# A hybrid DiT block on one core: the scan's quad loop written as four overlapping steps, one stage put between merge and transpose, splits and modulation of the FFN norm issued earlier, and the last output rows regrouped

## The chip, the cores and the metric

The kernel runs on one core of a Trainium2 chip. The metric is the device time of one execution in microseconds; the time before is 1929.78 us, the median of three runs (1927.39 to 1932.99). The core has five engines with queues of their own: TensorE (PE in the profile, PEld for its weight loads), VectorE (DVE), ScalarE (ACT), GpSimd (POOL, not used here) and SyncE (SP, which issues nearly all DMAs). Each engine runs its instructions in the order in which the program lists them.

## The reference

One layer of a diffusion block on 256 latent tokens and 256 context tokens of width 2048, all float32:

```
hl = rmsnorm(x) * (1 + sc_m) + sh_m
p  = hl @ w_in                      # SSD columns | z | pool | Fourier | three gates
y_ssd  = rmsnorm_per_group(ssd(p) * silu(z)) @ w_ssd_out
y_pool = pool(p), y_four = fourier(p) @ w_fourier
x = x + g_m * ((s0 * y_pool + s1 * y_four + s2 * y_ssd) @ w_out)      # s = sigmoid(gates)
x = x + g_f * swiglu(rmsnorm(x) * (1 + sc_f) + sh_f)                  # 2048 -> 5632 -> 2048
out = rmsnorm(x)
```

`ssd` is a bidirectional Mamba-2 scan over 32 heads in 4 groups, in chunks of 128 tokens; its initial states come from the context tokens. The six modulation vectors (sc, sh, g, each for mixer and FFN) are `silu(c) @ w_ada + b_ada`. Of the context only the scan states are needed, so its projection stops at the SSD columns.

## The kernel before

**Stages.** The product of tokens and weights is cut into *stages*. A stage is one weight tile of 2 x 128 rows by 512 columns (512 KB) and, as a rule, 12 matmuls of 128x128x512. The precision of float32 is kept by splitting both operands in a high and a low part: `split` (L123) makes `hi` with an ACT cast (L124) and `lo = raw - hi` with a DVE subtraction (L125), and `mm3` (L130) issues three matmuls (L131 hi x hi, L132 lo x hi, L133 hi x lo). So each stage asks one DMA of SP, one cast of ACT, one subtraction of DVE and 12 matmuls of PE.

**The order.** Nothing reorders the program; its order is made at build time by `stream` (L198). For stage i it issues loads up to stage i + LEAD + 3 and splits up to stage i + LEAD (LEAD is 2), then the stage's matmuls, then a helping of side work. Loaded tiles go through five buffers (`raw`), shared by the weight tiles and by the tiles of `w_ada`; split parts go through three (`whi`, `wlo`), or, for a stage that is *held*, through the large pool H (`hhi`, `hlo`). A buffer is loaded anew when ACT and DVE have read it; a split begins when PE has finished the stage that used the same part buffer.

**Side work** consists of generators in a list (`beside`). `side(room)` (L187) adds `room` to a credit (at most 3), and lets each generator take one step while the credit is above 0.2; a step gives back its own estimate of DVE time (`yield 1.2`). `need(key)` (L179) runs a generator to its end at once. The modulation vectors past the first are side work as well: `plan_ada` (L514) attaches *units* (a 512 KB tile of `w_ada`, one DVE multiply-add of 128x1024, L461) to stages.

**The places of the change, in the order of time.**
- *Scan* (`ssd`, L648): for each group of 8 heads a quad loop (L750 to L788) runs over two blocks b of 4 heads and two chunks t. Each quad makes 16 small ACT multiplications (L745, tiles `rh`) and 4 more (L757, tile `W`), four matmuls that sum the decays (L761), an ACT exponential (L767), a DVE product `W*E` (L768), and four matmuls with the values (L772); each block then adds the skip term (L778), is transposed (L784) and added into `y` (L787). The steps of one quad follow each other, one per helping of side work.
- *norm_y* (L1050): the group norm of the scan's output, started by `start_norm` 14 stages before the stages with `w_ssd_out` (called phase q here, L1079).
- *Phase q*: for each of four column blocks n, eight stages of gate, eight of `w_ssd_out`, then `merge(2, n)` (L953; DVE, L963 and L967, tile `mg`) and `to_feature(n)` (L1088), which transposes the merged block on PE (L1095) and splits it (L1098 ACT, L1099 DVE). `turn_m` asks for the merge with `need` and goes straight on.
- *Phase o* (`w_out`) and the *FFN norm*: the last block of `w_out` is arranged so that rows t = 0 end first (`mm_first`), while rows t = 1 (`mm_second`) and the first gate stages (`mm_gate0`, `mm_gate1`) follow in halves. `norm_ffn` (L1126) gives a diagonal matrix with 1/rms; `turn(n)` (L1137) transposes and scales a block by it on PE (L1141), modulates it with four DVE multiply-adds (L1144, 128x128 each), and splits it into `h2h` and `h2l`.
- *Last rows* (`last_rows`, L1314): the final 512 rows of `w_ffn_down`, in 8 pieces (column block n, half p). Pieces of n < 3 multiply the rows t = 0 only; after the last piece, `mm_piece` does n = 3 of t = 0 (in two spans of 256 columns), `finish(0)` (final norm and store of t = 0), all four blocks of t = 1, and `finish(1)`.

Of the kernel before, what the change touches and what calls it, by code (L numbers as in the profile page):

```python
# [72 lines left out]
class Stage:  # L73


    def __init__(self, src, n, mm, first=None, room=1.45, held=False):
        self.src, self.n, self.mm, self.first, self.room, self.held = src, n, mm, first, room, held
        self.after, self.extra = [], []
        self.raw = self.parts = None
# [3 lines left out]
def hybrid_block(ctx: ExitStack, tc, io):  # L83
# [114 lines left out]
    def stream():  # L198
        while at["run"] < len(stages):
            i = at["run"]  # L200
            st = stages[i]
            load_upto(i + LEAD + 4)
# [445 lines left out]
    def ssd(g):  # L648
# [87 lines left out]
        def operands(b, t):  # L736

            h0 = 8 * g + 4 * b
            rhs = []
            for d, r in enumerate((LE, GE)):  # L740
                for a in (dah, dal):
                    rh = Q([P, 4, P], F32R, nme="rh")
                    av = a[:, t, 32 * d + h0 : 32 * d + h0 + 4].bitcast(F32)
                    for i in range(4):
                        S.activation(rh[:, i, :], r, AF.Copy, scale=av[:, i : i + 1])  # L745
                    rhs.append((gt_r if d == 0 else lt_r, rh))
            return rhs

        yps = [None, None]
        for b in range(2):  # L750
            h0 = 8 * g + 4 * b
            yps[b] = aux([P, 2, 256])
            for t in range(2):
                rhs = operands(b, t)
                W = Q([P, 4, P], nme="W")
                for i in range(4):
                    S.activation(W[:, i, :], cbf[:, t, :], AF.Copy, scale=ddt[:, t, h0 + i : h0 + i + 1])  # L757
                yield 0.0
                seg = aux([P, 4, P])
                for n, (m, rh) in enumerate(rhs):  # L760
                    T.matmul(seg, m, rh, start=n == 0, stop=n == 3)  # L761
                for i in range(4):
                    V.scalar_tensor_tensor(W[:, i, :], cbb[:, t, :], ddt[:, t, 32 + h0 + i : 33 + h0 + i], W[:, i, :],
                                           ALU.mult, ALU.add)
                yield 1.1
                E = Q([P, 4, P], nme="E")
                S.activation(E, seg, AF.Exp)  # L767
                V.tensor_tensor(W, W, E, ALU.mult)  # L768
                yield 0.6
                for i in range(4):  # L770
                    h = 4 * b + i
                    T.matmul(yps[b][(h % 2) * 64 : (h % 2) * 64 + 64, i // 2, t * P : (t + 1) * P],  # L772
                             xl[:, t, h * HD : (h + 1) * HD], W[:, i, :], start=True, stop=True)
            yield 0.0
# [5 lines left out]
            yield 0.8  # L780
# [4 lines left out]
            yield 0.0  # L785
            yv = y[g][:, :, 256 * b : 256 * b + 256]
            V.tensor_tensor(yv, yv, ps, ALU.add)  # L787
            yield 0.6  # L788
# [261 lines left out]
    def norm_y():  # L1050
        S.activation(zss, zss, AF.Sqrt, bias=eps4, scale=1.0 / CH)
# [36 lines left out]
    def to_feature(n):  # L1088
        mh[n], ml[n] = H([P, 4, 256], F32R, nme="fth"), H([P, 4, 256], F32R, nme="ftl")
        for i in range(2):  # L1090
# [5 lines left out]
            yield 0.0  # L1096
            s2 = slice(2 * i, 2 * i + 2)
            S.activation(mh[n][:, s2, :], ps, AF.Copy, scale=0.5)  # L1098
            V.scalar_tensor_tensor(ml[n][:, s2, :], ps, 0.5, mh[n][:, s2, :].bitcast(F32), ALU.mult, ALU.subtract)  # L1099
        yield 1.2  # L1100
# [25 lines left out]
    def norm_ffn(t):  # L1126
# [10 lines left out]
        def turn(n):  # L1137
# [4 lines left out]
            for c in range(4):  # L1142
                kt = 4 * n + c
                V.tensor_scalar(hf[:, c, :], ps[:, c, :], Af[:, kt : kt + 1], Sf[:, kt : kt + 1], ALU.mult, ALU.add)  # L1144
# [13 lines left out]
    def phase_o(n):  # L1158
# [127 lines left out]
    oss = C([P, 2, 5], nme="oss")  # L1286

# [26 lines left out]
    def last_rows():  # L1314
# [9 lines left out]
        def block(t, n, i, cs, p):  # L1324
            if p == 0:
                ps[0] = acc((P, cs.stop - cs.start))
            hi, lo = pieces[2 * n + p]
            op = pair_op(ah[10:11], al[10:11])
            for k in range(2):
                kt = 2 * p + k  # L1330
                mm3(ps[0], *op(kt, t), hi[:, k, cs], lo[:, k, cs], kt == 0, kt == 3)
# [4 lines left out]
            V.tensor_tensor(tmp[:, cs], ps[0], gf[n][:, n % 2, cs], ALU.mult)  # L1336
# [24 lines left out]
        def mm_piece(n, p):  # L1361
            def mm(parts):
                pieces.append(parts)
                if n < 3:
                    block(0, n, 0, slice(0, CH), p)
                    return
                if p == 0:
                    return
                for t in range(2):
                    for m in range(4) if t else (3,):  # L1370
                        for i, cs in spans(m):
                            for q in range(2):
                                block(t, m, i, cs, q)
                    finish(t)
            return mm

        for n in range(4):
            for p in range(2):
                add(rows(io["w_ffn_down"], 40 + 2 * p, 2, n * CH, CH), CH, mm_piece(n, p),
                    first=first if n + p == 0 else None, room=0.3, held=True)  # L1380
# [36 lines left out]
    def start_norm():  # L1417
        need("ssd", "z0", "z1", "z2", "z3")
        spawn("Y", norm_y(), True)
    s_q = len(stages)  # L1420
    stages[s_q - 14].after.append(start_norm)
# [22 lines left out]
    plan_ada(u_all[:40], s_u, s_q)  # L1444
    plan_ada(u_all[40:], s_q, s_o + 10)
# [85 lines left out]
```

## Time and profile before

| | |
|---|---|
| median of three runs | 1929.78 us |
| the profiled execution | 1927.37 us, of which the span of its instructions is 1925.6 us |
| mean granted TensorE clock | 0.989 |
| busy: PE / DVE / ACT | 96% / 64% / 46% of the span |
| read from HBM | 405.56 MB, 212 GB/s over the span |

The profile's rows give, for each engine, an instruction's line in the kernel, its operation, `out<-in` tiles, shape and count. `[2.79 <-DVE mg L967]` behind a row of the timeline means that the engine stood idle for 2.79 us before it, and that the DVE instruction at L967, which writes a tile `mg`, released it. The table of waits sums these. In the table of stretches a row gives the busy time of each engine within the stretch, the granted clock (PEclk, 1.00 is full speed), and the DMA share and rate.

### The profile page before, as it was taken

The page shows a single profiled execution, that of the slowest core. Times are in us where ns is not written, and L with a number is a line of the kernel's source. Part 1 is how long each engine was busy: PE and PEld are TensorE (multiplying, and loading weights), DVE is VectorE, ACT ScalarE, POOL GpSimd, SP SyncE. Part 2 cuts the span into 40 slices and gives each one's busy share as a digit, 9 for nine tenths or more (in the row PEclk, how much of TensorE's full clock was granted, in tenths as well). Part 3 has the DMA queues.
Part 4 walks back from the last instruction along what each step waited for, and adds up shares of the span by engine and source line. Part 5 has one row for each costly group of instructions (what it writes and reads, how often), then busy time and mean ns, then how long its engine had stood idle before and what let it go on. Part 6 is the DMA issues. An engine that isn't in the chain of part 4 may idle for free. (4 is left out here: it accounts for less than half of the span.)

```text
span 1925.6 us, 23350 instructions
## 1 busy us (share of the span) xinstructions
PE 1850.3 (96%) x8808; PEld 1488.7 (77%) x8808; DVE 1237.2 (64%) x1509; ACT 880.0 (46%) x1314; POOL 0.2 (0%) x4
## 2 busy tenths in 40 slices
PE   5999999999999999998999997999999999999997
PEld 3667987777777877877778785888888888888886
DVE  4446785776675666778777655777755555555567
ACT  4223545835646547444334343444433444434444
POOL 0000000000000000000000000000000000000000
PEclk8999999999999999999999998999999999999999
DMA  9992432575666556778888763888856666656653
GB/s 328 358 330 77 114 111 71 170 232 178 219 207 191 170 176 197 242 232 306 294 296 286 252 203 93 279 280 289 274 193 190 195 189 187 193 193 191 193 189 131
DMA packets 211905, 409.20 MB, mean 213 GB/s; under 512 B 14672, under 2 KB 47568, under 8 KB 211792
## 3 DMA queue, kind: packets, MB, share of 16 engines
q1 hardware_dynamic: 211792, 407.71, 66.3%
q8 instruction: 69, 1.13, 0.2%
q14 instruction: 44, 0.36, 0.1%
HBM read 405.56 MB, written 2.10 MB: 212 GB/s over the span
## 5 line engine op out<-in xcount | busy, mean ns | idle before, releaser
L125 DVE TENSOR_TENSOR wlo<-raw,whi 128x1024 fp32r<-128x1024 f32 x544 | 664.8, 1223 | 599.6 <-ACT whi L124 595.9
L124 ACT CAST whi<-raw 128x1024 fp32r<-128x1024 f32 x544 | 570.0, 1052 | 768.3 <-PE acc L133 653.7
L131 PE MATMUL acc<-whi,h2h 128*128 128x512 f32 x700 | 274.4, 392 | 12.2 <-ACT whi L124 8.7
L132 PE MATMUL acc<-wlo,h2h 128*128 128x512 f32 x700 | 273.7, 391 | 0.5 <-DVE wlo L125 0.5
L133 PE MATMUL acc<-whi,h2l 128*128 128x512 f32 x700 | 273.8, 391 | 0.0
L131 PE MATMUL acc<-whi,lh 128*128 128x512 f32 x640 | 260.7, 407 | 1.8 <-ACT gt L947 1.7
L132 PE MATMUL acc<-wlo,lh 128*128 128x512 f32 x640 | 252.2, 394 | 2.4 <-DVE wlo L125 2.4
L133 PE MATMUL acc<-whi,ll 128*128 128x512 f32 x640 | 251.2, 392 | 0.0
L131 PEld LDWEIGHTS acc<-whi,h2h 128*128 128x128 f32 x700 | 132.1, 189 | 40.0 <-ACT whi L124 9.2
L133 PEld LDWEIGHTS acc<-whi,h2l 128*128 128x128 f32 x700 | 132.1, 189 | 27.9 <-DVE h2l L125 0.4
L461 DVE SCALAR_TENSOR_TENSOR adacc<-araw,sil,adacc 128x1024 f32<-128x1024 f32 x120 | 153.4, 1278 | 0.4 <-DMA araw<-w_ada 0.4
L132 PEld LDWEIGHTS acc<-wlo,h2h 128*128 128x128 f32 x700 | 132.0, 189 | 28.0 <-DVE wlo L125 1.0
L132 PEld LDWEIGHTS acc<-wlo,lh 128*128 128x128 f32 x640 | 121.5, 190 | 31.2 <-DVE wlo L125 5.5
L131 PEld LDWEIGHTS acc<-whi,lh 128*128 128x128 f32 x640 | 121.4, 190 | 30.8 <-issue 2.4
L133 PEld LDWEIGHTS acc<-whi,ll 128*128 128x128 f32 x640 | 121.1, 189 | 26.0
L131 PE MATMUL acc<-whi,ah 128*128 128x512 f32 x320 | 124.8, 390 | 0.0
L133 PE MATMUL acc<-whi,al 128*128 128x512 f32 x320 | 124.5, 389 | 0.0
L132 PE MATMUL acc<-wlo,ah 128*128 128x512 f32 x320 | 124.5, 389 | 0.0
L131 PE MATMUL acc<-hh,whi 128*128 128x512 f32 x256 | 105.0, 410 | 3.6 <-ACT whi L124 3.6
L132 PE MATMUL acc<-hl,whi 128*128 128x512 f32 x256 | 100.5, 393 | 0.0
L133 PE MATMUL acc<-hh,wlo 128*128 128x512 f32 x256 | 100.5, 392 | 0.0
L131 PEld LDWEIGHTS acc<-whi,ah 128*128 128x128 f32 x320 | 60.1, 188 | 12.4
(290 smaller groups left out, 2328.7 us busy)
## 6 DMA issues: line engine op xcount, KB each, us to landing
raw<-w_in SPq DMA_DIRECT2D x208, 512.0 KB, 4.3
araw<-w_ada SPq DMA_DIRECT2D x128, 512.0 KB, 4.7
raw<-w_ffn_gate SPq DMA_DIRECT2D x88, 512.0 KB, 3.8
raw<-w_ffn_up SPq DMA_DIRECT2D x88, 512.0 KB, 3.8
raw<-w_ffn_down SPq DMA_DIRECT2D x88, 512.0 KB, 3.7
raw<-w_ada SPq DMA_DIRECT2D x64, 512.0 KB, 9.3
raw<-w_ssd_out SPq DMA_DIRECT2D x32, 512.0 KB, 5.4
raw<-w_out SPq DMA_DIRECT2D x32, 512.0 KB, 4.7
```

The source lines that it names most:

```text
L124: S.copy(hi, src)
L125: V.tensor_tensor(lo, src, hi.bitcast(F32), ALU.subtract)
L131: T.matmul(out, ah, bh, start=first, stop=False)
L132: T.matmul(out, ah, bl, start=False, stop=False)
L133: T.matmul(out, al, bh, start=False, stop=last)
L461: V.scalar_tensor_tensor(a, self.raw, sil[:, kt : kt + 1], a, ALU.mult, ALU.add)
```

## The change

**Scan.** `operands`, `head_sums`, `scaled` and `products` are now the four steps of a quad, and one pass k of the new loop does `products` of quad k-3, `head_sums` of quad k-1, `scaled` of quad k-2 and `operands` of quad k, so that four quads are under way. Half of the small ACT multiplications (those with `dal`) become two DVE products of 128x512 for each quad. There are 10 passes for each group where there were 20 steps; the passes declare 14.2 us of credit in all, the steps 9.6. On ACT, within the third group of heads (tiles: `rh` and `W` as above, `whi` a stage's cast), before:

```order
L745 ACTIVATE rh_4151<-cc_73,dah_385 128x128 x4
L745 ACTIVATE rh_4156<-cc_73,dal_386 128x128 x4
L745 ACTIVATE rh_4161<-cc_73,dah_385 128x128 x4
L745 ACTIVATE rh_4166<-cc_73,dal_386 128x128 x4
L757 ACTIVATE W_4171<-cbf_3737,ddt_384 128x128 x4
L124 CAST whi_4178<-raw_4072 128x1024
L124 CAST whi_4207<-raw_4104 128x1024
L767 ACTIVATE E_4224<-aux_4194 128x512
```

And ACT after the change, in the second group of heads:

```order
L747 ACTIVATE rh_3664<-cc_73,dah_385 128x128 x4
L747 ACTIVATE rh_3671<-cc_73,dah_385 128x128 x4
L752 ACTIVATE W_3663<-cbf_3461,ddt_384 128x128 x4
L124 CAST whi_3686<-raw_3565 128x1024
L124 CAST whi_3704<-raw_3602 128x1024
L124 CAST whi_3724<-raw_3625 128x1024
L767 ACTIVATE E_3749<-aux_3654 128x512
L747 ACTIVATE rh_3753<-cc_73,dah_385 128x128 x4
```

Twelve small multiplications stand between two casts where twenty stood, and the exponential that follows (`E_3749`) belongs to the quad before.

**Merge and transpose.** `turn_m` waits, one helping at a time, until the merge has ended and lets one more stage pass; `to_feature` issues both groups of transposes together. `norm_y` is started 36 stages ahead of phase q and waits in the same way for the scan and the four z. On DVE at the end of the first block of phase q (`gt`, `mg`: merge; `wlo`: a stage's split; `adacc`: a unit; `ftl`: split of the transposed block), before:

```order
L963 SCALAR_TENSOR_TENSOR gt_7351<-gt_7351,acc_7296 128x512
L967 TENSOR_TENSOR mg_3408<-mg_3408,gt_7351 128x512
L963 SCALAR_TENSOR_TENSOR gt_7353<-gt_7353,acc_7297 128x512
L967 TENSOR_TENSOR mg_3408<-mg_3408,gt_7353 128x512
L125 TENSOR_TENSOR wlo_7517<-raw_7427,whi_7516 128x1024
L461 SCALAR_TENSOR_TENSOR adacc_7294<-araw_7429,sil_98,adacc_7294 128x1024
L1099 SCALAR_TENSOR_TENSOR ftl_7506<-aux_7507,fth_7505 128x512
L125 TENSOR_TENSOR wlo_7547<-raw_7448,whi_7546 128x1024
L1099 SCALAR_TENSOR_TENSOR ftl_7506<-aux_7537,fth_7505 128x512
```

And DVE at the same place after the change:

```order
L1001 TENSOR_TENSOR mg_3418<-mg_3418,gt_7187 128x512
L125 TENSOR_TENSOR wlo_7372<-raw_7293,whi_7371 128x1024
L461 SCALAR_TENSOR_TENSOR adacc_7351<-araw_7295,sil_98,adacc_7351 128x1024
L997 SCALAR_TENSOR_TENSOR gt_7189<-gt_7189,acc_7174 128x512
L1001 TENSOR_TENSOR mg_3418<-mg_3418,gt_7189 128x512
L125 TENSOR_TENSOR wlo_7395<-raw_7314,whi_7394 128x1024
L461 SCALAR_TENSOR_TENSOR adacc_7351<-araw_7316,sil_98,adacc_7351 128x1024
L125 TENSOR_TENSOR wlo_7425<-raw_7343,whi_7424 128x1024
L461 SCALAR_TENSOR_TENSOR adacc_7351<-araw_7345,sil_98,adacc_7351 128x1024
L125 TENSOR_TENSOR wlo_7460<-raw_7369,whi_7459 128x1024
L1138 SCALAR_TENSOR_TENSOR ftl_7444<-aux_7445,fth_7443 128x512
```

The splits of three stages now stand between the merge's last row and the first `ftl`. On PE the transposes come 4 stages after the block's end, where they came 1 and 2 stages after it. For the fourth block they come one stage ahead of the stage of phase o that reads them.

**Units.** 32 units of `w_ada` instead of 40 are attached ahead of phase q, and 64 instead of 56 to the 74 stages from phase q's start to the tenth stage of phase o.

**FFN norm.** The three held stages of the last `w_out` block get leads of 3, 4 and 5 (so their loads, too, are asked for earlier), which issues the splits of the second and third gate stage ahead of the norm; the four modulations of each `turn` go from DVE to ACT (an activation with scale and bias per partition). On ACT from the first norm on (`h2h`: cast of the modulated block; `junk`: sum of squares of rows t = 1; `r`: square root), before:

```order
L124 CAST whi_9295<-raw_9243 128x1024
L124 CAST h2h_9285<-h_9318 128x4x128
L1124 ACTIVATE junk_9331,xss_391<-x_9150 128x512
L1115 ACTIVATE r_9333<-r_9333,eps_75 128x1
L124 CAST h2h_9287<-h_9340 128x4x128
L124 CAST h2h_9289<-h_9352 128x4x128
L124 CAST h2h_9291<-h_9364 128x4x128
L124 CAST whi_9377<-raw_9255 128x1024
L124 CAST whi_9399<-raw_9293 128x1024
L124 CAST h2h_9285<-h_9410 128x4x128
L124 CAST whi_9423<-raw_9375 128x1024
```

And ACT from the first norm on after the change:

```order
L1183 ACTIVATE h_9231<-aux_9230,Sf_383,Af_382 128x128 x4
L124 CAST h2h_9204<-h_9231 128x4x128
L1163 ACTIVATE junk_9244,xss_391<-x_9055 128x512
L1154 ACTIVATE r_9246<-r_9246,eps_75 128x1
L1183 ACTIVATE h_9253<-aux_9252,Sf_383,Af_382 128x128 x4
L124 CAST h2h_9206<-h_9253 128x4x128
L1183 ACTIVATE h_9265<-aux_9264,Sf_383,Af_382 128x128 x4
L124 CAST h2h_9208<-h_9265 128x4x128
L1183 ACTIVATE h_9277<-aux_9276,Sf_383,Af_382 128x128 x4
L124 CAST h2h_9210<-h_9277 128x4x128
L124 CAST whi_9304<-raw_9162 128x1024
L1183 ACTIVATE h_9315<-aux_9314,Sf_383,Af_382 128x128 x4
```

The casts of the second and third gate stage (`whi_9295`, `whi_9377`) have gone from here to a place ahead of the norm; four modulations stand ahead of each cast of a block.

**Last rows.** Pieces of n < 2 multiply both rows t, n = 2 and n = 3 the rows t = 0; after `finish(0)` only n = 2 and n = 3 of t = 1 are left. Pieces of n < 2 are no longer held, and the first stages have more room for side work. The core of the diff:

```diff
-            split_upto(i + LEAD + 1)
+            split_upto(i + st.lead + 1)
...
-                    for i in range(4):
-                        S.activation(rh[:, i, :], r, AF.Copy, scale=av[:, i : i + 1])
+                    if a is dah:
+                        for i in range(4):
+                            S.activation(rh[:, i, :], r, AF.Copy, scale=av[:, i : i + 1])
+                    else:
+                        V.tensor_tensor(rh, bh(av, P), r.unsqueeze(1).to_broadcast([P, 4, P]), ALU.mult)
...
+        for k in range(10):
+            cost = 0.0
+            if 3 <= k < 7:
+                products(*its[k - 3], ops[k - 3][1])
+            if 1 <= k < 5:
+                segs[k - 1] = head_sums(*its[k - 1], *ops[k - 1])
+                cost += 1.1
+            if k in (6, 8):
+                turned_[k] = turned_y(yTs[k])
+            if 2 <= k < 6:
+                scaled(segs[k - 2], ops[k - 2][1])
+                cost += 0.6
+            if k < 4:
+                ops[k] = operands(*its[k])
+                cost += 1.2
+            if k in (5, 7):
+                yTs[k + 1] = skip((k - 5) // 2)
...
     def norm_y():
+        while not {"ssd", "z0", "z1", "z2", "z3"} <= ended:
+            yield 0.0
...
-                V.tensor_scalar(hf[:, c, :], ps[:, c, :], Af[:, kt : kt + 1], Sf[:, kt : kt + 1], ALU.mult, ALU.add)
+                S.activation(hf[:, c, :], ps[:, c, :], AF.Identity, bias=Sf[:, kt : kt + 1], scale=Af[:, kt : kt + 1])
...
             add(rows(io["w_out"], 2 * p, 2, 3 * CH, CH), CH, mm_first(p), held=True, room=0)
+            stages[-1].lead = p - n_o + 3
...
-                if n < 3:
-                    block(0, n, 0, slice(0, CH), p)
+                for t in range(2) if n < 2 else (0,):
+                    block(t, n, 0, slice(0, CH), p)
+                if n < 3 or p == 0:
                     return
...
+                finish(0)
+                for m in range(2, 4):
+                    for i, cs in spans(m):
+                        for q in range(2):
+                            block(1, m, i, cs, q)
+                finish(1)
...
-                need(f"m2{n}")
+                while f"m2{n}" not in ended:
+                    yield 0.0
+                yield 0.0
                 yield from to_feature(n)
...
-    plan_ada(u_all[:40], s_u, s_q)
-    plan_ada(u_all[40:], s_q, s_o + 10)
+    plan_ada(u_all[:32], s_u, s_q)
+    plan_ada(u_all[32:], s_q, s_o + 10)
```

More of the change, by code (lines that the diff above doesn't have):

```diff
@@ new lines, in operands @@
+                    if a is dah:
[3 more added lines that the diff above has]
+                        V.tensor_tensor(rh, bh(av, P), r.unsqueeze(1).to_broadcast([P, 4, P]), ALU.mult)
+                    rhs.append((gt_r if d == 0 else lt_r, rh))
+            for i in range(4):
+                S.activation(W[:, i, :], cbf[:, t, :], AF.Copy, scale=ddt[:, t, h0 + i : h0 + i + 1])
@@ new lines, in operands, with head_sums, scaled @@
+            return rhs, W
+        def head_sums(b, t, rhs, W):
+            h0 = 8 * g + 4 * b
+            seg = aux([P, 4, P])
+            for n, (m, rh) in enumerate(rhs):
+                T.matmul(seg, m, rh, start=n == 0, stop=n == 3)
+            for i in range(4):
+                V.scalar_tensor_tensor(W[:, i, :], cbb[:, t, :], ddt[:, t, 32 + h0 + i : 33 + h0 + i], W[:, i, :],
+                                       ALU.mult, ALU.add)
+            return seg
+        def scaled(seg, W):
+            E = Q([P, 4, P], nme="E")
+            S.activation(E, seg, AF.Exp)
+            V.tensor_tensor(W, W, E, ALU.mult)
@@ L775, in ssd, with products, skip @@
+        yps = [None, None]
+        def products(b, t, W):
+            if t == 0:
+                yps[b] = aux([P, 2, 256])
+            for i in range(4):
+                h = 4 * b + i
+                T.matmul(yps[b][(h % 2) * 64 : (h % 2) * 64 + 64, i // 2, t * P : (t + 1) * P],
+                         xl[:, t, h * HD : (h + 1) * HD], W[:, i, :], start=True, stop=True)
+        def skip(b):
             yT = Q([P, 2, 256], nme="yT")
@@ L784, in ssd, with into_y @@
                     T.transpose(ps[:, t, i * P : (i + 1) * P], yT[:, i, t * P : (t + 1) * P], ID)
-            yield 0.0
+            return ps
+        def into_y(b, ps):
             yv = y[g][:, :, 256 * b : 256 * b + 256]
             V.tensor_tensor(yv, yv, ps, ALU.add)
-            yield 0.6
+        its = [(b, t) for b in range(2) for t in range(2)]
+        ops, segs, yTs, turned_ = {}, {}, {}, {}
+        for k in range(10):
[15 more added lines that the diff above has]
+                yTs[k + 1] = skip((k - 5) // 2)
+                cost += 0.8
+            if k in (7, 9):
+                into_y((k - 7) // 2, turned_[k - 1])
+                cost += 0.7
+            yield cost
     lh, ll = [], []
@@ L1095, in to_feature @@
                     T.transpose(ps[:, k, t * P : (t + 1) * P], merged[n][:, t, c * P : (c + 1) * P], ID)
[L1096 removed]
+            pss.append(ps)
+        yield 0.0
+        for i in range(2):
             s2 = slice(2 * i, 2 * i + 2)
[L1098 to L1100 removed]
+            S.activation(mh[n][:, s2, :], pss[i], AF.Copy, scale=0.5)
+            V.scalar_tensor_tensor(ml[n][:, s2, :], pss[i], 0.5, mh[n][:, s2, :].bitcast(F32), ALU.mult, ALU.subtract)
+        yield 1.4
     x1 = [None] * 4
@@ L1325, in block @@
             if p == 0:
-                ps[0] = acc((P, cs.stop - cs.start))
+                ps[t] = acc((P, cs.stop - cs.start))
             hi, lo = pieces[2 * n + p]
@@ L1379, in last_rows @@
                 add(rows(io["w_ffn_down"], 40 + 2 * p, 2, n * CH, CH), CH, mm_piece(n, p),
-                    first=first if n + p == 0 else None, room=0.3, held=True)
+                    first=first if n + p == 0 else None, room=0.3 if n else 1.4, held=n > 1)
     def all_ssd():
@@ L1415, in hybrid_block @@
         phase_f(n)
-    def start_norm():
-        need("ssd", "z0", "z1", "z2", "z3")
-        spawn("Y", norm_y(), True)
     s_q = len(stages)
-    stages[s_q - 14].after.append(start_norm)
+    stages[s_q - 36].after.append(lambda: spawn("Y", norm_y(), True))
     for n in range(4):
```

49 lines of the change are left out of this document (10 added, 39 removed).

## The prediction

> **What bounds the kernel now.** I read the page first, then the stretches, PE's waits, and the timeline at the two places that wait most.
>
> ```profile
> PE 1850.3 (96%) x8808; PEld 1488.7 (77%) x8808; DVE 1237.2 (64%) x1509; ACT 880.0 (46%) x1314; POOL 0.2 (0%) x4
> ...
> L125 DVE TENSOR_TENSOR wlo<-raw,whi 128x1024 fp32r<-128x1024 f32 x544 | 664.8, 1223 | 599.6 <-ACT whi L124 595.9
> ...
> L461 DVE SCALAR_TENSOR_TENSOR adacc<-araw,sil,adacc 128x1024 f32<-128x1024 f32 x120 | 153.4, 1278 | 0.4 <-DMA araw<-w_ada 0.4
> ```
>
> PE is the bound: 1925.6 - 1850.3 leaves 75 us of idle time in the whole span, and the change removes no matmul work that matters. So it can win what PE loses in waits and what slow matmuls cost after a wait, no more. The stretches of the change (scan; norm_y's end, phase q and ten stages of phase o; FFN norm; last rows) beside two stretches in which PE never waits:
>
> ```profile
> 75.00:100.00 25.00, 25.00 (x190) 16.07 (x189) 8.87 (x17) 3.83 (x5) 0.00 (x0) 1.00 1.09 357
> 300.00:800.00 500.00, 489.35 (x2226) 385.32 (x2225) 342.13 (x452) 297.13 (x598) 0.00 (x0) 1.00 0.60 187
> 859.00:1090.00 231.00, 214.73 (x969) 173.12 (x968) 177.87 (x182) 92.43 (x110) 0.00 (x0) 0.98 0.85 292
> 925.00:950.00 25.00, 25.00 (x115) 20.64 (x115) 19.42 (x19) 11.50 (x13) 0.00 (x0) 1.00 0.91 322
> 1152.00:1188.00 36.00, 22.10 (x104) 17.36 (x103) 21.14 (x47) 9.45 (x16) 0.00 (x0) 0.82 0.19 59
> 1887.00:1926.00 39.00, 25.48 (x125) 21.11 (x123) 25.84 (x41) 14.89 (x32) 0.00 (x0) 0.91 0.32 113
> ```
>
> The columns are the stretch, its length, busy PE, PEld, DVE, ACT, POOL, then PEclk, DMA share, GB/s. PE idles 10.7 us in the scan, 16.3 in q, 13.9 at the norm, 13.5 at the end; nearly all the rest is the load at the start, which stays. Whom PE waits for after 300 us:
>
> ```profile
> PE aux L1095 <- DVE mg L967: 13.4, 8, 2.8
> PE acc L131 <- ACT whi L124: 9.3, 2, 8.7
> PE aux L772 <- DVE W L768: 6.5, 5, 2.4
> PE acc L131 <- ACT h2h L124: 4.2, 2, 3.5
> PE acc L132 <- DVE wlo L125: 3.6, 6, 0.8
> PE acc L131 <- ACT hhi L124: 3.4, 2, 2.0
> PE acc L131 <- ACT gt L947: 1.7, 1, 1.7
> PE acc L132 <- DVE hlo L125: 1.6, 2, 0.9
> PE aux L761 <- ACT rh L745: 1.3, 2, 0.7
> ```
>
> **Scan.** The waits at L772 (6.5), L761 (1.3) and behind a gate's activation (1.7) make 9.5 us. They arise because one quad's steps feed each other, and because a quad holds ACT with twenty small instructions before the next cast.
>
> ```profile
> L745 ACT ACTIVATE rh<-cc,dal 128x128 fp32r<-128x128 f32 x128 | 40.6, 391 | 0.0
> ```
>
> ```profile
> L768 DVE TENSOR_TENSOR W<-W,E 128x512 f32<-128x512 f32 x16 | 10.9, 683 | 0.0
> ```
>
> Removed from ACT: 128 x 0.32 (40.6/128, as they overlap) = 40.6 us. Added to DVE: 32 products of the shape of L768, 32 x 0.68 = 22 us, less 8 units that leave (8 x 1.28 = 10); DVE, busy 342 of 500 us, has room. A quad's block on ACT falls from 20 x 0.32 = 6.3 us to 3.8, and each product now uses what was made a pass earlier. In two places of the new order two passes stand only one stage apart; I leave 1.5 us for those. Net **-8**. Bounds: -11 (all 10.7 us go) to -3 (the DVE products delay splits as often as the waits go).
>
> **Phase q.** A boundary between column blocks:
>
> ```profile
> 955.32 0.39 PE L132 MATMUL acc<-wlo,lh 128*128 128x512 f32 x1
> 955.55 0.39 PE L133 MATMUL acc<-whi,ll 128*128 128x512 f32 x1
> 955.87 0.24 PE L485 MATMUL aux<-cc,adasb 32*128 32x32 f32 x1
> 958.90 0.30 PE L1095 MATMUL aux<-cc,mg 128*128 128x128 f32 x1 [2.79 <-DVE mg L967]
> 960.13 0.90 PE L1095 MATMUL aux<-cc,mg 128*128 128x128 f32 x3 [0.93 <-DVE mg L967]
> 960.68 0.78 PE L131 MATMUL acc<-whi,lh 128*128 128x512 f32 x1
> 961.26 0.63 PE L132 MATMUL acc<-wlo,lh 128*128 128x512 f32 x1
> ```
>
> PE waits for the merge, which DVE has just begun; afterwards matmuls start 0.58 us apart where they stood 0.23 apart. PEclk 0.98 over 231 us is 4.6 us of slow clock in the stretch, part of it during the idling; I take 1.2 us for each of three boundaries. With the transposes four stages (4 x 12 x 0.23 = 11 us) behind the block's end the merge, two helpings long, is over: 13.4 + 3.6 go. The norm_y work leaves the start of phase q, and with it some 2.7 us of the waits for splits. Against that, 8 more units lie in the stretch: DVE's 177.9 us grow by 10 and lose some 7 of norm_y, in a stretch shorter by 16: 181/215 = 84% for 77% now. The loads go from 292 GB/s x 231 us = 67.5 MB to 71.7 MB, 333 GB/s over 215 us. Before, PE ran 25 us without a wait at 322 GB/s here, and at 357 early on, so the rate exists; but the five buffers come free only as DVE reads them, and in the fourth block the transposed tile is read one stage after the transposes, with a split, a unit and two `ftl` on DVE in that stage (1.2 + 1.3 + 1.4 = 3.9 us against 2.8 of matmuls). I charge 4.2 us for all of this. Net 13.4 + 3.6 + 2.7 - 4.2 = **-15.5**; bounds -20 (no charge) to -8, the latter if 322 GB/s is the most that the loop of five buffers gives: 71.7 MB / 0.322 = 223 us for 231.
>
> **FFN norm.** PE from the first transposes to the first whole gate stage, 34.3 us, and ACT's part in it:
>
> ```profile
> 1152.90 3.81 PE L1141 MATMUL aux<-dg,x 128*128 128x128 f32 x32 [0.50 <-DVE dg L1132]
> ...
> 1187.17 0.63 PE L131 MATMUL acc<-whi,h2h 128*128 128x512 f32 x1
> ```
>
> ```profile
> 1159.39 0.30 ACT L1115 ACTIVATE r<-r,eps 128x1 f32<-128x1 f32 x1 [0.22 <-DVE r L1114]
> 1161.51 0.62 ACT L124 CAST h2h<-h 128x512 fp32r<-128x512 f32 x1 [1.83 <-DVE h L1144]
> 1164.16 0.62 ACT L124 CAST h2h<-h 128x512 fp32r<-128x512 f32 x1 [2.04 <-DVE h L1144]
> ...
> 1180.29 1.04 ACT L124 CAST whi<-raw 128x1024 fp32r<-128x1024 f32 x1 [4.32 <-PE acc L133]
> ```
>
> A `turn` takes 2.65 us, DVE and ACT in alternation. The wait of 8.7 us is for the third gate stage's cast, queued behind three turns; with that cast ahead of the norm it goes. (SP asks for these loads sooner, too; they wait for buffers in the same order, and nothing but loads is queued behind them.) Next late is ACT itself, now with four modulations to each cast. The nearest rows have the same operation with scale and bias:
>
> ```profile
> L525 ACT ACTIVATE cv<-xin,cwh 128x512 f32<-128x512 f32 x16 | 12.1, 804 | 0.0
> ...
> L525 ACT ACTIVATE cv<-cin,cwh 128x256 f32<-128x256 f32 x4 | 2.2, 589 | 0.0
> ```
>
> 0.215 us for 256 columns makes 0.48 for 128, about 0.45 in a row; four and a cast take 1.8 + 0.6 = 2.4 us. Along the new order: the root of rows t = 1 ends about 1158.9 (1159.69 before, and the first cast comes some 0.8 sooner); the second turn ends 1161.3, and PE, done with its transposes and two half stages at about 1159 (1152.9 + 3.8 + 2 x 1.4, a little overlapped), has waited 2.5 us. Then on ACT two turns, a cast of 1.0 and the first turn of t = 1: 1161.3 + 2 x 2.4 + 1.0 + 2.4 = 1169.5, while PE is done about 1164.5 (a half stage and two groups of transposes) and waits 5 us. Two half stages of 1.4 and a group of transposes of 0.9 end at 1173.2, at 1175 with 1.7 us for slow clock; the next cast needs the buffer that this frees, as the row at 1180.29 shows for before; cast and turn end at 1178.3; a half stage and 1 us of slow clock end at about 1181. That is **-6** against 1187.2. Bounds: five turns of the chain at 1.8 us (activations like L745's) give -9; at 0.8 for an activation (L525's at 512 columns) 3.8 a turn, +1.
>
> The Trainium skill, "ScalarE: Activation LUTs", Rules for kernel authors, says to do multiplications and additions on VectorE rather than ScalarE, which speaks against this edit. By operation alone the rows agree (1.8 us for four on ACT, 2.65 - 0.62 - hand-offs on DVE); what the edit buys is one hand-off less in a turn.
>
> The same section's estimate, 0.3 us and 0.83 ns an element, would make 0.41 us an activation, and the norm about -7.
>
> **Last rows.** PE's waits here (hhi 3.4, hlo 1.6) stand behind squares on ACT that wait for DVE. Stages of n < 2 now have 12 matmuls (2.8 us) for one split instead of 6, so they stop starving; but the casts of n = 3 then queue behind both squares of n = 1, and those behind six DVE operations of 0.69 and two splits: by the same adding up PE waits some 5 us there. The store of t = 1 still ends the run. Net **0**, bounds -3 to +3.
>
> **The sum.** -8 - 15.5 - 6 + 0 = -29.5. The profiled execution took 1927.4 us, 1.8 more than its span and 2.4 less than the median 1929.8; I put the difference to the median: **1900 us**.
>
> **Rivals.**
> - *The loop of five buffers limits phase q* at the 322 GB/s seen: 8 us there for 15.5, in all 1907.5. For it: DVE at 84%, and ACT and DVE are the only ones to free buffers. Against: 357 GB/s earlier. 0.2.
> - *ACT becomes the norm's bound*, 3.8 us a turn: +1 for -6, 1907. For it: the L525 row at 512 columns, and the rule above. Against: its row at 256 columns. 0.08.
> - *All waits go*: -11 - 20 - 9 - 3 = -43, 1887. Against: one queue per engine always leaves a next one late. 0.1.
> - *Slower*: the loads don't speed up at all. If DVE, always behind, frees buffers only fast enough for 275 GB/s, the stretch takes 71.7/0.275 = 261 us, +30 for 231, and 30 - 8 - 6 = +16: 1946. It decides below 285 GB/s (252 us). For it: 292 GB/s is today's mean. Against: today's mean includes PE's own waits, and 322 was held. 0.04.
> - *Clock*. After waits of at most 2.8 us the matmuls were slow; the Trainium skill, "TensorE: Matmul & The Clock Gate", Part 1, has the clock fall only after an idle window of some 3.4 us. If the three waits that I leave at the norm cost no clock save the longest, its term is -8 and the time 1898; 0.05, as two waits (2.79 and 0.93) with little between them did slow the clock here.
>
> **How the numbers follow.** Forecast (1891 to 1905) 0.49, the rivals as above. A measurement can tell 0.3%, 5.8 us, from no change. Below 1924 lie the forecast and all rivals but the slower one: faster 0.92. Slower 0.04; same 0.04, for a buffer loop between the two prices. The range goes from 1886, all waits gone, to 1914.5, where the first two rivals add up (1900 + 7.5 + 7).
>
> **What would show it.** Right: no wait at the transposes of phase q, PEclk 1.00 there, over 330 GB/s; waits at L772's place under 2 us; at the norm three waits of about 2.5, 5 and 2.5 us for ACT's casts, gate stages whole after some 28 us for 34; about 5 us of waits for hhi and hlo at the end. Wrong: waits for `wlo` or `whi` of over 8 us in phase q, or an idle PE of over 12 us at the norm.

## The result, and the profile after

The changed kernel takes 1902.4 us (median of four runs, 1901.1 to 1905.5) against 1928.6 us, a ratio of 0.9862 (95% interval 0.9842 to 0.9883); the forecast was 1900. The profiled execution took 1902.28 us, its span is 1900.5 us, the granted clock 0.992. The page, for the rows shown of before:

```profile
PE 1845.0 (97%) x8796; PEld 1483.7 (78%) x8796; DVE 1247.2 (66%) x1508; ACT 855.0 (45%) x1216; POOL 0.2 (0%) x4
...
L125 DVE TENSOR_TENSOR wlo<-raw,whi 128x1024 fp32r<-128x1024 f32 x548 | 669.4, 1223 | 564.9 <-ACT whi L124 559.9
...
L461 DVE SCALAR_TENSOR_TENSOR adacc<-araw,sil,adacc 128x1024 f32<-128x1024 f32 x120 | 153.4, 1278 | 2.1 <-DMA araw<-w_ada 2.0
```

PE's idle time has gone from 75 us to 55.5. The stretches of the change, in the order scan, phase q with ten stages of phase o, norm, last rows, with the columns as before:

```profile
300.00:800.00 500.00, 496.24 (x2289) 393.54 (x2288) 366.01 (x502) 271.66 (x488) 0.00 (x0) 1.00 0.60 183
845.00:1071.00 226.00, 215.74 (x963) 171.08 (x962) 185.45 (x184) 89.59 (x105) 0.00 (x0) 0.98 0.92 321
...
1134.00:1162.00 28.00, 20.49 (x101) 16.63 (x102) 8.96 (x15) 17.83 (x44) 0.00 (x0) 0.88 0.14 38
1862.00:1901.00 39.00, 25.17 (x109) 19.89 (x107) 26.55 (x40) 16.60 (x32) 0.00 (x0) 0.85 0.30 108
```

The scan idles 3.8 us for 10.7. Phase q still idles 10.3 us of the 16.3, though it loads 321 GB/s for 292. PE's waits after the start-up name the new cause:

```profile
PE acc L131 <- ACT h2h L124: 6.2, 3, 2.3
PE acc L132 <- DVE wlo L125: 5.4, 10, 0.8
PE acc L131 <- ACT hhi L124: 3.4, 1, 3.4
PE acc L131 <- ACT gt L981: 3.3, 2, 1.6
PE acc L131 <- ACT fth L1137: 2.1, 1, 2.1
PE aux L1180 <- DVE dg L1171: 1.7, 1, 1.7
PE acc L133 <- DVE ftl L1138: 1.3, 1, 1.3
PE aux L1132 <- DVE mg L1001: 1.1, 1, 1.1
```

The 13.4 us for `mg` have shrunk to one wait of 1.1, and those at L772 and L761 (now L777 and L759) are gone. In their place stand ten small waits for `wlo`, nine of them in phase q, and two at the fourth block of phase q (`fth`, `ftl`).

The main matmuls (L131 to L133) stand in the same number and order in both programs up to the last rows, so the two traces can be aligned on them. The difference of their starts, read at the borders of the parts (phase q begins with its first gate stage, 842.5 us in the changed kernel; its end is read after the twelfth stage of phase o, where the difference has settled):

| part | forecast, us | measured, us |
|---|---|---|
| start-up (nothing changed there) | 0 | -1.7 |
| scan, to the start of phase q | -8 | -9.5 |
| phase q, to the twelfth stage of phase o | -15.5 | -7.6 |
| FFN norm | -6 | -7.1 |
| last rows and end | 0 | +0.8 |
| sum | -29.5 | -25.1 |

So the total came out near the forecast although its largest term came out at about half. The experiments look for the 8 us that are missing there, and for what made the other terms.

Who holds the casts of ACT in phase q is the sharpest view: ACT's waits of the changed kernel from 845 to 1090 us.

```profile
ACT whi L124 <- DMA raw<-w_ssd_out: 46.3, 28, 3.8
ACT whi L124 <- DMA raw<-w_in: 39.1, 20, 3.5
ACT whi L124 <- PE acc L133: 15.4, 9, 2.1
ACT whi L124 <- DMA raw<-w_out: 13.2, 7, 4.0
```

A cast that waits for PE (a part buffer still in use) is ahead of PE; one that waits for a load is late. In the same span the kernel before has the two the other way round:

```profile
ACT whi L124 <- PE acc L133: 67.2, 42, 3.3
ACT whi L124 <- DMA raw<-w_ssd_out: 16.5, 9, 2.9
ACT whi L124 <- DMA raw<-w_in: 16.4, 8, 3.2
ACT whi L124 <- DMA raw<-w_out: 0.3, 1, 0.3
```

98.6 us of ACT's time now go into waiting for loads, 33.2 before. The fourth block shows what that does, ACT first, then PE:

```profile
1052.20 1.05 ACT L124 CAST whi<-raw 128x1024 fp32r<-128x1024 f32 x1 [4.04 <-DMA raw<-w_out]
1054.77 1.04 ACT L124 CAST whi<-raw 128x1024 fp32r<-128x1024 f32 x1 [1.52 <-DMA raw<-w_out]
1055.72 1.08 ACT L1137 ACTIVATE fth<-aux 128x512 fp32r<-128x512 f32 x2
```

```profile
1056.36 0.80 PE L131 MATMUL acc<-whi,fth 128*128 128x512 f32 x1 [2.09 <-ACT fth L1137]
1058.92 0.79 PE L133 MATMUL acc<-whi,ftl 128*128 128x512 f32 x1 [1.34 <-DVE ftl L1138]
```

The eviction `fth`, which needs no load, stands in ACT's queue behind two casts that do, and PE waits for it; then matmuls take 0.80 us for 0.39, and the granted clock is 0.50 until 1063 us.

### The profile page after: what moved, and what is told of

It reads as the page before. It is cut to its first block, busy times and chain, and to the rows that moved or that the text cites. A ratio compares the mean times of both kernels' runs of the same rounds, so it can differ in the third digit from the quotient of the medians.

```text
span 1900.5 us, 23216 instructions
## 1 busy us (share of the span) xinstructions
PE 1845.0 (97%) x8796; PEld 1483.7 (78%) x8796; DVE 1247.2 (66%) x1508; ACT 855.0 (45%) x1216; POOL 0.2 (0%) x4
## 4 chain that ended last, share of the span: by engine, by line
PE 81%; DMA 7%; DVE 5%; ACT 4%; issue 2%; SPq 1%; DVEq 0%; ACTq 0%
PE acc L131 23%; PE acc L133 23%; PE acc L132 23%; DMA raw<-w_ssd_out 4%; ACT whi L124 2%; PE aux L314 2%; DVE wlo L125 1%; DMA raw<-w_in 1%; DVE adacc L461 1%; DMA raw<-w_out 1%; PE aux L131 1%; PE aux L132 1%; PE aux L133 1%; PE aux L683 1%; PE aux L759 1%
## 5 line engine op out<-in xcount | busy, mean ns | idle before, releaser
L131 PE MATMUL acc<-whi,h2h 128*128 128x512 f32 x700 | 273.6, 391 | 4.4 <-ACT h2h L124 4.4
L133 PE MATMUL acc<-whi,h2l 128*128 128x512 f32 x700 | 273.1, 390 | 0.0
L131 PE MATMUL acc<-whi,lh 128*128 128x512 f32 x640 | 256.7, 401 | 3.5 <-ACT gt L981 3.3
L133 PE MATMUL acc<-whi,ll 128*128 128x512 f32 x640 | 249.7, 390 | 0.0
L131 PEld LDWEIGHTS acc<-whi,h2h 128*128 128x128 f32 x700 | 131.5, 188 | 31.8 <-ACT h2h L124 5.0
L133 PEld LDWEIGHTS acc<-whi,h2l 128*128 128x128 f32 x700 | 131.5, 188 | 28.3 <-DVE h2l L125 0.9
L131 PEld LDWEIGHTS acc<-whi,lh 128*128 128x128 f32 x640 | 120.2, 188 | 31.5 <-ACT gt L981 4.1
L133 PEld LDWEIGHTS acc<-whi,ll 128*128 128x128 f32 x640 | 120.1, 188 | 25.3
L131 PE MATMUL acc<-whi,ah 128*128 128x512 f32 x336 | 131.0, 390 | 0.0
L133 PE MATMUL acc<-whi,al 128*128 128x512 f32 x336 | 130.7, 389 | 0.0
L132 PE MATMUL acc<-wlo,ah 128*128 128x512 f32 x336 | 130.7, 389 | 0.0
L131 PE MATMUL acc<-hh,whi 128*128 128x512 f32 x256 | 104.9, 410 | 3.6 <-ACT whi L124 3.6
L133 PE MATMUL acc<-hh,wlo 128*128 128x512 f32 x256 | 100.5, 392 | 0.0
L133 PEld LDWEIGHTS acc<-whi,al 128*128 128x128 f32 x336 | 63.1, 188 | 13.1
```

The costliest lines, as they stand in the source:

```text
L131: T.matmul(out, ah, bh, start=first, stop=False)
L132: T.matmul(out, ah, bl, start=False, stop=False)
L133: T.matmul(out, al, bh, start=False, stop=last)
```

## Experiments

Theory: five raw buffers limit phase q (a buffer comes free when DVE has read it, and its next load needs some 5 us to land). Rivals: the transfer engines themselves, or the order of work on ACT and DVE.

**A control, and six buffers.** Memory for the sixth buffer comes from the pool of short-lived tiles, so that pool is cut by itself first.

```diff
-HS, QS = 28, 17
+HS, QS = 28, 15
```

> Control for the next run: the changed kernel with 15 buffers of 2 KB instead of 17 in the pool of short-lived tiles, everything else the same. No wait of the trace ends on that pool, so every theory gives the changed kernel's 1902 us, +-3. More than that would make this run, and not the changed kernel, the one that the six-buffer run is held against.

Measured: 1903.8 us, ratio 0.9871 (0.9857 to 0.9886), the same as the changed kernel.

```diff
-LEAD, RAWS, PARTS = 2, 5, 3
-HS, QS = 28, 17
+LEAD, RAWS, PARTS = 2, 6, 3
+HS, QS = 28, 15
```

> The changed kernel with six raw buffers of 512 KB instead of five, and 15 short-lived ones to make room. Theory of the loop: in the output projection of the scan's branch (phase q) a load waits for one of five buffers, and five of 512 KB at the landing times of 5 to 6 us bring 321 GB/s; a sixth lets the loop run up to the 330 GB/s that start-up shows, the 72.5 MB of the stretch take 220 us instead of 226, and the waits for wlo, whi and fth (8.8 us) fall to 3: 1895 to 1898. Theory of the transfer engines: they are at a share of 0.92 in the stretch and full at 330 GB/s in start-up, so a sixth buffer is only a longer queue: the landing median goes from 5.4 to 6.4 us and the time stays at 1900 to 1904. Theory of VectorE's order (82% busy, splits behind other work): no change either, and the landing median stays as well, because the sixth buffer is not used.

Measured: **1885.9 us**, ratio 0.9776 (0.9761 to 0.9791), 18 us below the control and the fastest kernel of the study, against 4 to 7 below the changed kernel expected. Aligned with the control, 15.7 us of it lie in phase q, and 2.4 in the start-up. ACT's waits with six buffers (845 to 1090 us), then the 207 us from the fifth stage of its phase q to the twelfth of phase o:

```profile
ACT whi L124 <- PE acc L133: 88.7, 53, 2.1
ACT whi L124 <- DMA raw<-w_ssd_out: 17.7, 11, 2.7
ACT whi L124 <- DMA raw<-w_out: 4.0, 2, 2.2
ACT whi L124 <- DMA raw<-w_in: 2.1, 1, 2.1
```

```profile
854.00:1061.00 207.00, 206.24 (x960) 168.74 (x958) 179.98 (x179) 89.69 (x107) 0.00 (x0) 1.00 0.94 341
```

The casts wait for PE again, PE idles 0.8 us, and the core loads 341 GB/s with DVE busy 87%. So neither the transfer engines nor DVE held the changed kernel at 321. The expectation was too small because it took some 330 GB/s of the start-up for the ceiling.

**The kernel before with six buffers.**

> The kernel before with six raw buffers instead of five and 15 short-lived tiles instead of 17, nothing else. It asks what the change itself takes off where the loop of buffers does not bind. The changed kernel with the same six buffers ran 1885.9 us. Theory: phase q of the kernel before lost its time at the transposes' waits (a cast and a sum between merge and transpose), which a sixth buffer does not touch, and the buffers were a limit only of the changed kernel, whose q loads 321 GB/s where this one loads 292: 1922 to 1929, so that the change is worth 36 to 43 us with six buffers, and its term in q is the forecast -15.5 or more. Rival: the sixth buffer helps the kernel before as much as the changed one (18 us), because its own late casts in q came from the loop too: 1909 to 1914, and the change is worth 23 to 28 us with six buffers as with five.

Measured: 1925.7 us, ratio 0.9996 (0.9985 to 1.0007): no change, and PE's first wait of phase q is what it was.

```profile
PE aux L1095 <- DVE mg L967: 12.3, 8, 2.3
```

The buffers limited only the changed kernel: the merge's waits had hidden them. With six buffers on both sides the change is worth 40 us, 22.7 of them in phase q, where five buffers leave 7.6. The loop costs 15 us; the forecast had charged 4.2. No run took the added stage out of the first three boundaries; that it ends the merge's waits rests on the waits themselves, 12.3 us here and none for `mg` in phase q of the changed kernel with six buffers.

**Fewer bytes in the stretch.** First the units as before, 40 ahead of phase q:

```diff
-    plan_ada(u_all[:32], s_u, s_q)
-    plan_ada(u_all[32:], s_q, s_o + 10)
+    plan_ada(u_all[:40], s_u, s_q)
+    plan_ada(u_all[40:], s_q, s_o + 10)
```

> The changed kernel with the plan of the modulation's weights as it was before: 40 units ahead of phase q and 56 from there on, instead of 32 and 64. Theory of the loop: the stretch of 226 us loads 130 buffers instead of 138, 6% less, so that at 321 GB/s bytes would need 213 us and TensorE's 215.7 decide: the waits of 10 us fall to 2 to 5, and the scan, which has 198 GB/s and VectorE at 72%, takes the eight units for nothing or for 1 to 2 us: 1893 to 1898. Rival: the scan's stretch pays (VectorE's units of 1.2 us each stand ahead of the scan's sums, 8 x 1.2 = 10 us): 1902 to 1908.

Measured: 1893.9 us, ratio 0.9827 (0.9812 to 0.9841). Aligned with the changed kernel, the scan loses 4.2 us and phase q wins 14.3. So the change's own plan of units costs it some 8 us net: it moved 4 MB into the one stretch that was about to be short of buffers.

Then the same 64 units over ten more stages:

```diff
-    plan_ada(u_all[32:], s_q, s_o + 10)
+    plan_ada(u_all[32:], s_q, s_o + 20)
```

> The changed kernel with the last 64 of the 96 units of the modulation's weights spread over 84 stages (to the 20th stage of the output projection) instead of 74. The stretch of 226 us then carries 68.4 MB instead of 72.5, 318 GB/s at TensorE's 215.7 us. If bytes limit the stretch (by the loop of buffers or by the transfer engines), its waits go from 10 us to 2 to 4, and nothing new comes up in the output projection, which has 218 GB/s now: 1894 to 1897. If the waits come from the order of work on ScalarE and VectorE (a cast that waits for a load stands ahead of the merges' and transposes' evictions), eight units fewer take off at most a tenth of them: 1901 to 1903. A third outcome: the modulation's last units come too late for the FFN norm, which then waits: over 1904.

Measured: 1899.0 us, ratio 0.9839 (0.9823 to 0.9855). Phase q wins 15.5 us, as bytes or buffers would have it, but 9.9 come back in phase o, which I had not expected. There ACT stops behind the last units' sum and the residual:

```profile
1083.75 1.14 ACT L124 CAST ahi<-adacc 128x512 fp32r<-128x512 f32 x2 [2.49 <-DVE adacc L461]
1087.05 0.63 ACT L1163 ACTIVATE junk<-x 128x512 f32<-128x512 f32 x1 [2.17 <-DVE x L1161]
```

**The added stage at the fourth block.**

```diff
-                yield 0.0
+                if n < 3:
+                    yield 0.0
                 yield from to_feature(n)
```

> The changed kernel, in which the last of the four merges (n = 3) goes to its transposes without the added stage between them; the other three keep it. Theory of the last boundary: where the output projection begins, the aligned matmuls gave back 7.2 us against the kernel before, with waits of 2.1 us for fth and 1.3 us for ftl and a granted clock of 0.86 there, because the added stage puts the last transposes' evictions behind casts that wait for loads; without it 3 to 6 us come back: 1896 to 1899. Rival: the loads are late there in any case, and without the stage the transposes wait for the merge instead (mg, 1.5 to 2.5 us at each place before): 1901 to 1904.

Measured: 1899.7 us, ratio 0.9850 (0.9835 to 0.9865), 2.7 us below the changed kernel, whose runs (1901.1 to 1905.5) overlap with these (1897.2 to 1902.5); the alignment of the two profiles gives -4.1 us at this boundary and +1.2 at the norm. By the alignment the stage costs a few us there, as expected, but it isn't the bulk: with six buffers the same boundary, its stage kept, waits 0.8 us.

**The modulation's engine.** Back on VectorE, the sooner splits kept:

```diff
-                S.activation(hf[:, c, :], ps[:, c, :], AF.Identity, bias=Sf[:, kt : kt + 1], scale=Af[:, kt : kt + 1])
+                V.tensor_scalar(hf[:, c, :], ps[:, c, :], Af[:, kt : kt + 1], Sf[:, kt : kt + 1], ALU.mult, ALU.add)
```

> The changed kernel with the four modulations of a turn of the FFN norm back on VectorE (as in the kernel before), the sooner splits kept. The changed kernel's norm waits three times for ScalarE's casts (2.07, 1.82, 2.30 us) and takes 28 us from the first transposes to full stages. Theory of the hand-off: on ScalarE the modulation needs no change of engine ahead of the cast, and four of them take 1.50 us; on VectorE they come after the splits and evictions that VectorE has there, and each turn costs 0.5 to 1 us more over seven turns, of which three end on TensorE's path: 1904 to 1906. Rival by the Trainium skill (ScalarE: Activation LUTs, Rules for kernel authors: products and sums belong on VectorE): with the modulation on VectorE a turn is shorter and the three waits fall by a half, 1898 to 1900. Third: the sooner splits alone made the norm's gain of 7 us: within 1 us of 1902.

Measured: 1911.0 us, ratio 0.9917 (0.9902 to 0.9932), 9 us slower. 6.2 us of it lie at the norm; 2.2 are a longer start-up, where nothing differs. Two turns there, on ACT of this run and of the changed kernel:

```profile
1148.26 0.62 ACT L124 CAST h2h<-h 128x512 fp32r<-128x512 f32 x1 [2.04 <-DVE h L1183]
1150.91 0.62 ACT L124 CAST h2h<-h 128x512 fp32r<-128x512 f32 x1 [2.04 <-DVE h L1183]
```

```profile
1143.91 1.50 ACT L1183 ACTIVATE h<-aux,Sf,Af 128x128 f32<-128x128 f32 x4
1145.44 0.62 ACT L124 CAST h2h<-h 128x512 fp32r<-128x512 f32 x1
1145.97 1.50 ACT L1183 ACTIVATE h<-aux,Sf,Af 128x128 f32<-128x128 f32 x4
1147.50 0.62 ACT L124 CAST h2h<-h 128x512 fp32r<-128x512 f32 x1
```

A turn takes 2.65 us with the hand-off and 2.06 without. So 6.2 of the norm's 7.1 us are the engine's, and 0.9 the sooner splits'. The Trainium skill ("ScalarE: Activation LUTs", Rules for kernel authors) would have the product on VectorE; this trace agrees on the four operations alone (1.36 us there, 1.50 on ScalarE) and not on the turn.

**Two and two.**

```diff
-                S.activation(hf[:, c, :], ps[:, c, :], AF.Identity, bias=Sf[:, kt : kt + 1], scale=Af[:, kt : kt + 1])
+                if c % 2:
+                    V.tensor_scalar(hf[:, c, :], ps[:, c, :], Af[:, kt : kt + 1], Sf[:, kt : kt + 1], ALU.mult, ALU.add)
+                else:
+                    S.activation(hf[:, c, :], ps[:, c, :], AF.Identity, bias=Sf[:, kt : kt + 1], scale=Af[:, kt : kt + 1])
```

> The changed kernel with two of a turn's four modulations on ScalarE and two on VectorE. If the turn's own length (four on one engine 1.50 us, then the cast 0.6) sets the three waits of the norm, two and two beside each other take 0.75 us off each turn on the path: 1899 to 1901. If the waits come from what stands ahead of the turn on either engine (the split of the last weights, the residual's sums and square), nothing changes or the later engine of the two decides: 1902 to 1905.

Measured: 1909.2 us, ratio 0.9906 (0.9891 to 0.9921), as slow as all four on VectorE. The engines did not work side by side but in turns, each waiting for the other's last operation:

```profile
1145.15 0.45 ACT L1186 ACTIVATE h<-aux,Sf,Af 128x128 f32<-128x128 f32 x1
1146.32 0.46 ACT L1186 ACTIVATE h<-aux,Sf,Af 128x128 f32<-128x128 f32 x1 [0.72 <-DVE h L1184]
1147.26 0.62 ACT L124 CAST h2h<-h 128x512 fp32r<-128x512 f32 x1 [0.48 <-DVE h L1184]
```

I took the shared result tile for the cause and gave each engine its own, with six buffers:

```diff
-            hf = Q([P, 4, P], nme="h2")
+            ha, hv = Q([P, 2, P], nme="h2"), Q([P, 2, P], nme="h2")
...
+            for c in range(2):
+                ka, kv = 4 * n + c, 4 * n + 2 + c
+                S.activation(ha[:, c, :], ps[:, c, :], AF.Identity, bias=Sf[:, ka : ka + 1], scale=Af[:, ka : ka + 1])
+                V.tensor_scalar(hv[:, c, :], ps[:, 2 + c, :], Af[:, kv : kv + 1], Sf[:, kv : kv + 1], ALU.mult, ALU.add)
...
+            split(h2h[n][:, 0:2, o], h2l[n][:, 0:2, o], ha)
+            split(h2h[n][:, 2:4, o], h2l[n][:, 2:4, o], hv)
```

> Six raw buffers and 15 short-lived tiles (1885.9 us by itself), and the norm's turn on two tiles: channels 0 and 1 of each turn modulated on ScalarE in one tile, 2 and 3 on VectorE in another, each split by itself. With one tile for both, the two engines took turns (0.5 us from one to the other, a turn every 2.63 us, against 2.06 on ScalarE alone and 2.65 on VectorE alone). Theory that the tile was what made them take turns: a turn takes 2 x 0.375 on ScalarE and two casts of 0.35, 1.45 to 1.6 us, some 0.5 less over the eight turns: 1881 to 1884. Rival: the second cast waits for VectorE, which has the first half's difference ahead of the next turn's modulations, the turn stays at 2.1 to 2.3 us: 1885 to 1888.

Measured: 1886.9 us, ratio 0.9787 (0.9766 to 0.9808), no better than six buffers alone, and the turn takes 2.18 us. That theory falls: they still take turns.

```profile
1126.00 0.45 ACT L1183 ACTIVATE h<-aux,Sf,Af 128x128 f32<-128x128 f32 x1
1126.93 0.46 ACT L1183 ACTIVATE h<-aux,Sf,Af 128x128 f32<-128x128 f32 x1 [0.48 <-DVE h L1184]
```

The rows name an instruction of the other engine as the releaser, so the turns are an order that the program's semaphores impose; the runs don't show that the chip would need it. What both still read is one PSUM tile of 2 KB a partition, and the small tables of scale and bias (`Af`, `Sf`). The Trainium skill ("PSUM — Partial Sum Buffer", PSUM bank collisions raise a hardware error) says that two engines must be kept off one bank at the same time, reads included, which would make them take turns; a run with two PSUM tiles, which would tell it from the tables, was not made.

**The scan's order, and its relief of ScalarE.** One quad behind the other, with the new products on VectorE; then the old loop whole.

```diff
-        for k in range(10):
-            cost = 0.0
...
+        for b in range(2):
+            for t in range(2):
+                rhs, W = operands(b, t)
+                yield 0.0
+                seg = head_sums(b, t, rhs, W)
+                yield 1.1
+                scaled(seg, W)
+                yield 0.6
+                products(b, t, W)
```

> The changed kernel with the scan's four quads one behind the other again (operands, sums, product with the exponential, head products, then the turn of y), the second half of the operands still on VectorE as in the change. The aligned matmuls put the scan's gain at about 10 us, and the waits for W and E at its products are gone. Theory of the order: the pipeline took the waits away, so that nearly all of the 10 us comes back: 1909 to 1914. Theory of the relief: ScalarE's 25 us less of work took them away, the order is worth little, 1902 to 1905.

Measured: 1904.2 us, ratio 0.9872 (0.9849 to 0.9895); up to the start of phase q +1.4 us.

```diff
-                    if a is dah:
-                        for i in range(4):
-                            S.activation(rh[:, i, :], r, AF.Copy, scale=av[:, i : i + 1])
-                    else:
-                        V.tensor_tensor(rh, bh(av, P), r.unsqueeze(1).to_broadcast([P, 4, P]), ALU.mult)
+                    for i in range(4):
+                        S.activation(rh[:, i, :], r, AF.Copy, scale=av[:, i : i + 1])
```

> The changed kernel with the whole of the scan's quad loop as in the kernel before: one quad behind the other, and both halves of the operands on ScalarE. It gives the size of the scan's term with the rest of the change in place: 1910 to 1914 if the 10 us that the aligned matmuls show are all its own (forecast 8, bounds 3 to 11). By the theory of the order this run and the one ahead of it are within 2 us of each other; by the theory of the relief this one is 6 us or more above it.

Measured: 1921.3 us, ratio 0.9965 (0.9955 to 0.9976); up to the start of phase q +17.9 us. PE's waits at the same products, in the first of the two runs and in the second:

```profile
PE aux L777 <- DVE W L768: 3.0, 3, 1.3
```

```profile
PE aux L774 <- DVE W L765: 12.9, 7, 3.2
```

The theory of the order falls: 16.5 of the 17.9 us are the operands that went to VectorE (ScalarE is busy 855.6 us with them there, 890.9 with them on ScalarE). The pipeline alone, with the operands on ScalarE, was not run. What stays open is why the old loop costs 18 us in the changed kernel, where the step from the kernel before to the changed one brought 9.5 here; the earlier `norm_y` and eight units fewer in the scan are the other differences.

**The last rows as before** (`last_rows` of the kernel before in the changed one):

> The changed kernel with the last rows grouped as in the kernel before. Forecast 0 for this part (bounds -3 and +3); the aligned matmuls show +0.8, with 4.5 us of waits for hhi and hlo instead of 5.0. Theory that it makes no difference: 1901 to 1904. Theory that the group at the end costs what the alignment shows: 1900.5 to 1901.5. Theory that the old order would now be caught by later splits: over 1905.

Measured: 1901.0 us, ratio 0.9860 (0.9842 to 0.9878): no difference that the times can tell; aligned, the old grouping ends 1.8 us sooner. The wait that the new grouping leaves is 3.41 us long, that of the old one 1.99:

```profile
1879.89 0.80 PE L131 MATMUL acc<-hhi,ah 128*128 128x512 f32 x1 [3.41 <-ACT hhi L124]
1881.15 0.79 PE L132 MATMUL acc<-hlo,ah 128*128 128x512 f32 x1 [0.46 <-DVE hlo L125]
```

```profile
1869.61 0.80 PE L131 MATMUL acc<-hhi,ah 128*128 128x512 f32 x1 [1.99 <-ACT hhi L124]
1870.87 0.80 PE L132 MATMUL acc<-hlo,ah 128*128 128x512 f32 x1 [0.47 <-DVE hlo L125]
```

## Why the prediction was right, and where it was not

*The total* was right, partly by luck: phase q brought 7.9 us less than forecast, and the scan 1.5, the norm 1.1 and the start-up 1.7 more, the last of these by chance, since nothing changed there.

*Phase q* is the step that failed, and within it the 4.2 us charged for the loop of buffers. The gain before that charge, 19.7 us, was nearly right: 22.7 with six buffers on both sides. The charge was 15, which puts the term just outside its bound of -8. The prediction had the rival that came true in hand, five buffers at 322 GB/s and 8 us for 15.5, and gave it 0.2; the stretch ran at 321 and brought 7.6. What misled was the argument that 357 GB/s had been seen. Of the 17 loads issued in that stretch of the start-up, 15 are tiles of `w_ada` for the first modulation vector, which lie in the large pool H and are read by PE itself (L314); only two went through the five buffers. So the 357 GB/s tell what the transfer engines brought there, and nothing of the loop. With 333 GB/s asked for by its own sum, and 322 the most that the loop had held, the rival should have been the forecast. And eight units were priced as DVE work and bytes (10 us on DVE with room), where taking them out again is worth 14.3 us in phase q. Of the signs named for it, the waits for `wlo` and `whi` (5.4 us) stayed under the 8 that were to mean "wrong", while 321 GB/s and a clock of 0.98 missed "over 330" and "1.00".

*Scan.* The size was nearly right (-9.5 for -8), the reason only half: with the operands on VectorE, the overlap of the four steps is worth some 1.4 us, and putting the operands back on ScalarE costs 16.5. Whether the overlap alone would have ended the waits was not run. The prediction named both and did not say which.

*FFN norm.* Right in mechanism and nearly in size, -7.1 for -6. Three waits were forecast at 2.5, 5 and 2.5 us; the middle one came out far shorter:

```profile
1144.06 0.50 PE L131 MATMUL acc<-whi,h2h 128*128 128x512 f32 x1 [2.07 <-ACT h2h L124]
1151.17 0.50 PE L131 MATMUL acc<-hhi,h2h 128*128 128x512 f32 x1 [1.82 <-ACT h2h L124]
1160.07 0.50 PE L131 MATMUL acc<-whi,h2h 128*128 128x512 f32 x1 [2.30 <-ACT h2h L124]
```

The turn was put at 2.4 us and took 2.06, because four activations in a row take 1.50 us, 0.375 each, where 0.45 was taken. The rival with ScalarE as the bound is out.

*Last rows.* Forecast 0 with some 5 us of waits for `hhi` and `hlo` left; 4.4 were left, and undoing the part changes nothing that the times can tell.

*Clock.* The rival taken from the Trainium skill ("TensorE: Matmul & The Clock Gate", Part 1), that the clock falls only after some 3.4 us of idling, does not fit: the row at 1056.36 has a matmul of 0.80 us, where 0.39 is usual, behind a wait of 2.09 us. The length of one wait is not what decides here: the clock fell to 0.50 after the norm's waits of 2.07 and 1.82 us too, and stayed at 1.00 after the longer one of 2.30. In this trace it changes at 1056.20, 1063.03, 1144.95, 1148.37, 1151.78 and 1155.19 us, all whole multiples of 3.41 us apart. The 3.41 us ahead of the three falls hold 1.93, 2.07 and 1.82 us of idle PE; the wait of 2.30 us lies across such a border, 0.84 us ahead of it and 1.46 behind, and no fall follows. After the start-up (230 us on) the fourteen traces of this case have 73 falls, each behind such a stretch with at least 1.65 us of idle PE, and a fall behind every stretch with more than 1.96. That fits a clock that falls when PE idles more than about half of one stretch; no run was made to test it.

## What to carry to other kernels

When a change takes a wait off the engine that bounds the kernel, work out the load rate that the stretch then asks for, and take the highest rate held through the same buffers, not the highest in the trace, as what the buffers give. A look at which way the casts wait (for the engine that uses them, or for the loads) tells how near that limit is. An operation moved beside its consumer on one engine can pay although it is slower there; splitting it over two engines, which then took turns, did not.

## What the runs showed of the hardware that was not expected

The core loaded 341 GB/s for 207 us beside matmuls at full clock, with one more buffer of 512 KB; with five it stayed at 321, and a load landed in 5 to 6 us either way (`w_ssd_out`: 6.1 and, in the control, 5.7 with five, 5.7 with six). TensorE's granted clock changed on a grid of 3.41 us; idling of 1.82 us within one step of the grid was followed by half the clock, a wait of 2.30 us spread over two steps was not. Where one engine waits for the last operation of the other, ScalarE and VectorE stand idle 0.48 to 0.53 us at each hand-over, and that ate what the split of the modulation could have won.
